# Eight experts in order of their load: three of them in 64-slot turns with the high and low parts in one stationary tile

## The chip, the cores and the metric

The kernel runs on one core of a Trainium2 chip. The metric is the device time of one execution in microseconds (us); lower is better. The median of three runs of the kernel before is 2497.24 us (2496.4 to 2498.56).

## The reference, cut to what matters

The model is two blocks of layers over 256 tokens of width 1024. The change lies in the mixture of experts of the first block:

```python
def moe_swiglu(xn, w_router, w_gate, w_up, w_down):     # N_EXPERTS 8, TOP_K 2, D_FF_EXPERT 3584
    logits = (xn @ w_router).astype(jnp.float32)
    top_v, top_i = lax.top_k(logits, TOP_K)
    top_w = jax.nn.softmax(top_v, axis=-1)
    gates = jnp.sum(jax.nn.one_hot(top_i, N_EXPERTS) * top_w[..., None], axis=-2)
    y = jnp.zeros_like(xn)
    for e in range(N_EXPERTS):
        y = y + gates[..., e:e + 1] * swiglu(xn, w_gate[e], w_up[e], w_down[e])
    return y
```

Each token goes to two of eight experts, so 512 places are filled, 64 for an expert on average. Counted with the reference's own inputs, experts 0 to 7 get 62, 71, 60, 74, 68, 59, 54 and 64 tokens.

## The kernel before, in words

All products are made of float32r matmuls on TensorE (PE). A number is split into a high part (rounded to float32r) and a low part (what is left), and a product takes three matmuls: high x high, high x low and low x high (`mm3`, lines 320 to 324). Weights come from HBM in chunks of 1 MB (`Stream`, lines 219 to 290). One chunk is 128 partitions x 2048 columns, and is split as two *parts* of 1024 columns: ScalarE (ACT) copies a part into `whi` (line 272), then VectorE (DVE) subtracts that copy from the raw weights and writes `wlo` (line 273). There are five pairs of `whi` and `wlo`, so a part can be converted only when PE is done with the part five before it. The raw chunks of the experts have 4 + 3 + 4 = 11 buffers. SyncE (SP) issues all these loads on one queue, in order of use, each when a buffer is free.

The router (line 816) gives each token a slot in each of its two experts; `weigh` makes the gates and the largest load, which is read into registers. `gather` (line 886) multiplies the tokens with one-hot tiles, for two experts at a time: 32 matmuls of 256 columns, after which `xgh` and `xgl` hold the transposed rows of up to 128 slots of either expert.

`experts` (line 913) takes the experts 0 to 7 one after the other, each over 128 slots. An expert has 14 *steps* j of 256 hidden columns. A step has two chunks of up and gate weights (four parts), whose 24 matmuls of 512 moving columns go into a bank `mm`; the slots' rows are the stationary operand, the weights move. Then ACT takes the silu of one half (line 941), DVE multiplies it by the other (line 942), PE transposes the result (line 946, two matmuls), and ACT and DVE split it into `hh` and `hl`. The down projection of the step before (one chunk, two parts, 12 matmuls into `acc`) follows in the program. At the end of an expert `acc` is split into `yh` and `yl` and put back to the tokens by eight matmuls (line 962) and four additions on DVE (line 964). In the last expert the parts are converted in halves of 512 columns (line 268).

A scheduler at build time sets the order of each engine's instructions, across the program's own order. On the chip each engine keeps to that order: an instruction that waits holds up all that stand behind it on its engine. If any load is over 128, a second pass over all eight experts takes the slots from 129 on (line 986); it does not run with these loads.

Of the kernel before, what the change touches and what calls it, by code (L numbers as in the profile page):

```python
# [11 lines left out]
F32 = mybir.dt.float32  # L12
# [10 lines left out]
NB = T // P  # L23
# [153 lines left out]
# ---------------------------------------------------------------- constants of the shapes  # L177

def constants():
# [12 lines left out]
    c["before"] = np.stack([np.triu(np.ones((P, P)), 1), np.ones((P, P))], axis=1)  # L192
    c["iota"] = np.broadcast_to(np.arange(1, P + 1)[None, :], (P, P))
    a = np.arange(P)
# [22 lines left out]
# ---------------------------------------------------------------- the program  # L217

class Stream:
    """Weights in the order of use: loaded ahead, then split into two float32r parts."""  # L220

    def __init__(self, prog, plans, raw_bufs, hl_bufs, raw_pool, hl_pool):
        self.nc = prog.nc
        self.items, self.parts, self.first = [], [], []
        for ap, plan in plans:
            offs, _ = offsets(plan)
            for c, o in zip(plan, offs):
                self.first.append(len(self.parts))
                step = max(c.kt // 2, 1)
                self.parts += [(len(self.items), k, step) for k in range(0, c.kt, step)]  # L230
                self.items.append((ap, c, o))
        self.first.append(len(self.parts))
# [6 lines left out]
    def widen(self, pool, bufs, until):  # L239
        """More room for raw chunks up to the one of the key `until`."""  # L240
# [5 lines left out]
    def fill(self, most=None):  # L246
        while self.n_raw < min(len(self.items), most or len(self.items)):
# [6 lines left out]
            step = f if self.n_raw else f // 2  # L254
            for c0 in range(0, f, step):
                self.nc.sync.dma_start(t[:, c0:c0 + step], bass.AP(tensor=ap.tensor, offset=ap.offset + o + c0, ap=[[f, P], [1, step]]))
# [24 lines left out]
    def get(self, *keys):  # L281
        """The rows of the next chunks, 128 at a time: a list of hi, lo [128, n]."""
# [10 lines left out]
class Program:  # L293
    RAW, HL = 4, 5

    def __init__(self, tc, io, stop=None, dump=None):
# [3 lines left out]
        self.turns = {}  # L300

    # -- small helpers

    def pool(self, name, bufs=1, **kw):
        """A tile pool whose tiles wait only for the earlier users of their own bytes."""
# [3 lines left out]
    def banks(self, **uses):  # L309
        """Which of the eight banks of PSUM each use takes in turn."""  # L310
# [24 lines left out]
    def inv_rms(self, ss, n, scale):  # L335
        """(ss * scale + eps) ** -0.5 on [128, n] sums of squares."""
# [7 lines left out]
    def row_rms(self, h, b, r):  # L344
        """r[:, b] = 1 / rms of the rows of block b of h."""
# [9 lines left out]
    def transposed(self, dst, src, b, kt):  # L355
        """dst hi/lo [128, kt, 256][:, :, block b] from src [128, kt * 128]."""
# [12 lines left out]
    def turned_h(self, gain, out, by_half=False):  # L369
        """h times the gain, transposed and split."""  # L370
# [7 lines left out]
    def normed_T(self, gain, by_half=False, pool=None):  # L378
        """h times the gain, transposed and split, and the rows' 1 / rms, which the products take after."""
# [7 lines left out]
    def row_of(self, pool, r):  # L387
        """r [128, 2] of the tokens as a row on every partition, [128, 256]."""
# [7 lines left out]
    def lin_tok(self, xT, keys, n, use):  # L396
        """x @ W for one column range: use(b, psum[:, :n])."""
# [7 lines left out]
    def lin_feat(self, xT, key):  # L405
        """(x @ W).T for 256 columns: psum [128, 2, 256]."""
# [26 lines left out]
    def down(self, acc, hT, keys, first, last, scale=None, store=False):  # L433
        """acc[b][n] += hT.T @ W for chunks of rows; hT(k) gives hi, lo [128, 256]."""
# [15 lines left out]
    def residual(self, b, n, ps, scale):  # L450
        """h += ps, or ps times a number for each token."""
# [6 lines left out]
    def at(self, name):  # L458
        """True where a debugging run ends."""
# [5 lines left out]
    # -- the whole  # L465

    def run(self):
        nc, io = self.nc, self.io
        with ExitStack() as st, ExitStack() as self.later, \
# [7 lines left out]
            self.w = Stream(self, [(io["w1"], plan_first()), (io["we"], sum((plan_expert(e) for e in range(NE)), [])),  # L477
# [5 lines left out]
            nc.vector.memset(self.mhalf, -0.5)  # L483
# [1006 lines left out]
```

## Time and profile before

| | us |
|---|---|
| median of 3 runs | 2497.24 |
| fastest, slowest run | 2496.4, 2498.56 |
| span of the profiled execution | 2493.5 |
| PE busy | 2462.6 (99%) |
| PE weight loads busy | 2066.8 (83%) |
| DVE busy | 1893.2 (76%) |
| ACT busy | 1560.4 (63%) |
| DMA, share of 16 engines (largest queue) | 64.2% |

The profile has no other time of that execution than its span; the span is 3.7 us under the median of the runs. The busy shares are means over stages with different limits: the experts, from about 575 to 1582 us, are the longest stage, and the one in which DMA and DVE are busiest. A busy PE is one with a matmul in flight; how fast it goes is read from the distance between the starts of matmuls.

### The profile page before, as it was taken

To read this page: it belongs to the slowest core of one execution; us is meant where nothing else is said; L and a number is where in the kernel's file an instruction comes from. 1 tells how busy PE (TensorE), PEld (TensorE's weight loads), DVE (VectorE), ACT (ScalarE), POOL (GpSimd) and SP (SyncE) were. 2 spreads that over 40 slices of the span, in tenths; PEclk is the share of its full clock that TensorE was granted. 3 is DMA by queue.
4 is the path that set the end of the run, shared out by engine and by line. 5 is a ranking of instruction groups with operands and counts; after the bars stand their busy time and mean duration, and the time that the engine had idled before them with its cause. 6 is when DMAs were issued, how large, how long until landed. Compare 5 with 4: busy or idle time off the path is not lost. (4 is left out here: it accounts for less than half of the span.)

```text
span 2493.5 us, 35325 instructions
## 1 busy us (share of the span) xinstructions
PE 2462.6 (99%) x13280; PEld 2066.8 (83%) x13280; DVE 1893.2 (76%) x2926; ACT 1560.4 (63%) x2560; POOL 63.6 (3%) x105
## 2 busy tenths in 40 slices
PE   8999999999999999999999999899999999999999
PEld 6978998888878888878887877698779989877998
DVE  5656557659999988898888898878676567867655
ACT  6446556657877777777777777645745554564544
POOL 0000000000000000000000000100000000100000
PEclk9999999999999999999999999999999999999999
DMA  7445555557999898989898988534255554424553
GB/s 280 165 167 206 186 186 186 197 232 297 367 347 363 327 364 341 359 336 367 341 365 336 363 344 338 146 126 175 102 176 204 186 171 133 176 105 172 194 187 108
DMA packets 88244, 605.75 MB, mean 243 GB/s; under 512 B 10336, under 2 KB 12000, under 8 KB 17152
## 3 DMA queue, kind: packets, MB, share of 16 engines
q1 hardware_dynamic: 85648, 593.96, 64.2%
q0 software_dynamic: 2416, 9.44, 1.7%
q8 instruction: 107, 1.75, 0.3%
q14 instruction: 73, 0.60, 0.1%
HBM read 602.31 MB, written 1.05 MB: 242 GB/s over the span
## 5 line engine op out<-in xcount | busy, mean ns | idle before, releaser
L273 DVE TENSOR_TENSOR wlo<-wraw,whi 128x512 fp32r<-128x512 f32 (+1 forms) x1656 | 1382.9, 875 | 383.6 <-ACT whi L272 365.5
L272 ACT ACTIVATE whi<-wraw 128x512 fp32r<-128x512 f32 (+1 forms) x1656 | 1205.3, 776 | 471.0 <-PE mm L323 211.3
L322 PE MATMUL mm<-xth,whi 128*128 128x256 f32 x1296 | 366.2, 283 | 0.0
L324 PE MATMUL mm<-xth,wlo 128*128 128x256 f32 x1296 | 364.9, 282 | 0.9 <-DVE wlo L273 0.9
L323 PE MATMUL mm<-xtl,whi 128*128 128x256 f32 x1296 | 365.8, 282 | 0.0
L323 PE MATMUL mm<-wlo,xgh 128*128 128x512 f32 x896 | 356.9, 398 | 2.8 <-DVE wlo L273 1.8
L322 PE MATMUL mm<-whi,xgh 128*128 128x512 f32 x896 | 355.1, 397 | 0.0
L324 PE MATMUL mm<-whi,xgl 128*128 128x512 f32 x896 | 354.3, 395 | 0.0
L324 PE MATMUL acc<-whi,hl 128*128 128x512 f32 x792 | 316.7, 401 | 0.3 <-DVE hl L328 0.3
L323 PE MATMUL acc<-wlo,hh 128*128 128x512 f32 x792 | 314.8, 398 | 0.0
L322 PE MATMUL acc<-whi,hh 128*128 128x512 f32 x792 | 297.0, 397 | 0.5 <-ACT hh L327 0.5
L323 PEld LDWEIGHTS mm<-xtl,whi 128*128 128x128 f32 x1296 | 244.3, 189 | 4.2 <-issue 2.5
L322 PEld LDWEIGHTS mm<-xth,whi 128*128 128x128 f32 x1296 | 244.4, 189 | 2.9 <-issue 1.1
L324 PEld LDWEIGHTS mm<-xth,wlo 128*128 128x128 f32 x1296 | 244.5, 189 | 1.8 <-DVE wlo L273 1.1
L323 PE MATMUL mm<-wlo,xth 128*128 128x512 f32 (+2 forms) x592 | 232.9, 394 | 0.8 <-DVE wlo L273 0.8
L322 PE MATMUL mm<-whi,xth 128*128 128x512 f32 (+2 forms) x592 | 232.7, 393 | 0.3 <-ACT xth L327 0.2
L324 PE MATMUL mm<-whi,xtl 128*128 128x512 f32 (+2 forms) x592 | 229.8, 389 | 0.4 <-DVE xtl L328 0.4
L323 PEld LDWEIGHTS mm<-wlo,xgh 128*128 128x128 f32 x896 | 168.4, 188 | 48.4 <-DVE wlo L273 9.5
L322 PEld LDWEIGHTS mm<-whi,xgh 128*128 128x128 f32 x896 | 168.3, 188 | 39.6
L324 PEld LDWEIGHTS mm<-whi,xgl 128*128 128x128 f32 x896 | 168.4, 188 | 38.5
L322 PEld LDWEIGHTS acc<-whi,hh 128*128 128x128 f32 x792 | 148.8, 188 | 34.7 <-ACT hh L327 1.8
L324 PEld LDWEIGHTS acc<-whi,hl 128*128 128x128 f32 x792 | 148.7, 188 | 33.9 <-DVE hl L328 1.9
(375 smaller groups left out, 2602.1 us busy)
## 6 DMA issues: line engine op xcount, KB each, us to landing
wraw<-in_we_dram SPq DMA_DIRECT2D x336, 1024.0 KB, 5.5
wraw<-in_w_dram SPq DMA_DIRECT2D x218, 1024.0 KB, 4.8
wraw<-in_w_dram SPq DMA_DIRECT2D x4, 912.0 KB, 5.0
wraw<-in_w_dram SPq DMA_DIRECT2D x6, 512.0 KB, 3.7
bias<-in_rel_rows_dram POOLq DMA_DIRECT2D x4, 768.0 KB, 4.6
gain<-in_norm_ffn_dram POOLq DMA_DIRECT2D x2, 512.0 KB, 5.9
gn<-in_ret_gn_dram SPq DMA_DIRECT2D x4, 256.0 KB, 3.5
gain<-in_norm_ple_dram POOLq DMA_DIRECT2D x2, 512.0 KB, 6.0
```

The costliest lines, as they stand in the source:

```text
L272: self.nc.scalar.activation(h, src, AF.Copy)
L273: self.nc.vector.tensor_tensor(l, src, h.bitcast(F32), op=ALU.subtract)
L322: mm(out, l[0], r[0], start=start, stop=False)
L323: mm(out, l[0], r[1], start=False, stop=False)
L324: mm(out, l[1], r[0], start=False, stop=stop)
```

## The change: what it does

The experts are taken in *turns*. Turn 0 is always expert 0, and its weights are loaded as before. The other seven are ranked on the chip by their load; turns 2, 3, 5 and 6 take the four largest in falling order, turns 1, 4 and 7 the three smallest. Which expert a turn takes is read from SBUF into seven registers of SP, and each of the 294 loads of turns 1 to 7 has its address from such a register. Slots and gates are reordered by turn.

Turns 0, 2, 3, 5 and 6 are computed as before, over 128 slots (wide). Turns 1, 4 and 7 have room for 64 slots (narrow): the stationary tile holds the high parts of 64 slots in its first 64 columns and the low parts in the others, and a product is two matmuls (tile x `whi`, tile x `wlo`), so a step has 16 + 8 matmuls instead of 24 + 12. Rows 0 to 63 and 64 to 127 of the result must then be added. For `mm`, ACT copies the whole bank to SBUF (`cp`), and four float32 matmuls of 64 columns with `fold` (two identities on top of each other) add the two halves and transpose at once; silu, product and split then work on 128 x 128. For `acc` the one-hot tile has both halves, so putting the tokens back adds them. `gather` takes the turns in groups (0), (1, 2), (3, 4), (5, 6), (7). The second pass would run if a load were over its room (128 or 64).

```diff
+WIDE = (True, False, True, True, False, True, True, False)
+GROUPS = ((0,), (1, 2), (3, 4), (5, 6), (7,))
...
 # Stream.fill
-                self.nc.sync.dma_start(t[:, c0:c0 + step], bass.AP(tensor=ap.tensor, offset=ap.offset + o + c0, ap=[[f, P], [1, step]]))
+            if c.key[0] in ("eu", "ed"):
+                e = self.expert[c.key[1]] if c.key[1] else 0
+                src = ap[e:e + 1] if isinstance(e, int) else ap[bass.ds(e, 1)]
+                self.nc.sync.dma_start(t[:, :f], src[:, o:o + P * f].rearrange("o (p f) -> (o p) f", p=P))
...
 # router, weigh
+            nc.vector.tensor_copy(loads, total)
+            nc.vector.scalar_tensor_tensor(key, loads, float(NE), self.turn[:, 2], op0=ALU.mult, op1=ALU.subtract)
+            nc.vector.memset(key[:, 0:1], 1e6)
+            nc.vector.tensor_tensor(perm, pairs(key, 0), pairs(key, 1), op=ALU.is_gt)
+            nc.vector.tensor_reduce(rank, perm, axis=AX.X, op=ALU.add)
+            nc.vector.tensor_tensor(perm, pairs(rank, 0), pairs(self.turn[:, 0], 1), op=ALU.is_equal)
+            for i, t in enumerate((self.turn[:, 2], loads)):
+                nc.vector.tensor_tensor(part[:, 0], perm, pairs(t, 0), op=ALU.mult)
+                nc.vector.tensor_reduce(picked[:, i], part[:, 0], axis=AX.X, op=ALU.add)
+            nc.vector.tensor_copy(which, picked[:, 0])
+            for i in range(1, NE):
+                self.expert[i] = nc.values_load(which[0:1, i:i + 1], (mybir.EngineType.SP,), min_val=0, max_val=NE - 1)
...
+            def by_turn(i, t):
+                nc.vector.tensor_tensor(part, t[:, :, None, :].to_broadcast([P, NB, NE, NE]),
+                                        perm[:, None].to_broadcast([P, NB, NE, NE]), op=ALU.mult)
+                nc.vector.tensor_reduce(in_turn[:, i], part, axis=AX.X, op=ALU.add)
...
 # gather, of a group with a narrow turn (its last)
+            nc.scalar.activation(flat(xg[0][:, ks])[:, :, :cut], flat(ps)[:, :, :cut], AF.Copy)
+            if nw:
+                nc.vector.tensor_tensor(xg[1][:, ks, 0], ps[:, :, 0], xg[0][:, ks, 0].bitcast(F32), op=ALU.subtract)
+            nc.vector.tensor_tensor(xg[0][:, ks, nw, 64:], ps[:, :, nw, 64:], xg[0][:, ks, nw, :64].bitcast(F32), op=ALU.subtract)
...
 # experts
+            def product(out, x, wk, start, stop):
+                if wide[e]:
+                    self.mm3(out, x, wk, start, stop)
+                else:
+                    nc.tensor.matmul(out, x[0], wk[0], start=start, stop=False)
+                    nc.tensor.matmul(out, x[0], wk[1], start=False, stop=stop)
...
+                else:
+                    hT[j] = (hh,)
+                    cp = self.work.tile([P, 512], F32, name="cp", tag="xs", bufs=3)
+                    nc.scalar.activation(cp, ps, AF.Copy)
+                    tp = self.bank("tp")[:, :256].rearrange("p (c s) -> p c s", s=64)
+                    for c in range(4):
+                        nc.tensor.matmul(tp[:, c], cp[:, c * P:(c + 1) * P], self.fold, start=True, stop=True)
+                    sg = self.work.tile([P, 2, 64], F32, name="sgn", tag="xs", bufs=3)
+                    nc.scalar.activation(sg, tp[:, :2], AF.Silu)
+                    nc.vector.tensor_tensor(sg, sg, tp[:, 2:], op=ALU.mult)
+                    self.split_psum(hh[:, :, :64], hh[:, :, 64:], sg)
```

On ACT, one step of an expert in the middle of the stage reads so before (`sg` is the silu, `hh` the split of the step's result):

```order
L272 ACTIVATE whi<-wraw 128x1024 x4
L941 ACTIVATE sg<-mm 128x256
L272 ACTIVATE whi<-wraw 128x1024 x2
L327 ACTIVATE hh<-tp 128x256
L272 ACTIVATE whi<-wraw 128x1024 x3
```

and so in turn 4 of the change (`cp` is the copy of the bank, `sgn` the silu):

```order
L288 ACTIVATE whi<-wraw 128x1024 x5
L1025 ACTIVATE cp<-mm 128x512
L1030 ACTIVATE sgn<-tp 128x128
L288 ACTIVATE whi<-wraw 128x1024
L344 ACTIVATE hh<-sgn 128x2x64
```

The silu now stands right behind the copy, with PE's four `fold` matmuls between the two, and no conversion of weights between them. Counted through the stream, `cp` stands here behind the second part after the last of its own step, and so do the last five steps of turn 1; in the first seven steps of turn 1 it stands behind the fifth, with a conversion before the silu. In turn 7 it stands behind the second, again with a conversion before the silu.

On PE, around the transposes of a step before (`tp<-ident,sg`):

```order
L322 MATMUL acc<-whi,hh 128x512 x2
L323 MATMUL acc<-wlo,hh 128x512
L946 MATMUL tp<-ident,sg 128x128 x2
L324 MATMUL acc<-whi,hl 128x512
L323 MATMUL acc<-wlo,hh 128x512
```

and around the `fold` matmuls of turn 4 of the change:

```order
L994 MATMUL mm<-wlo,xgh 128x512
L993 MATMUL acc<-whi,hh 128x512 x2
L994 MATMUL acc<-wlo,hh 128x512
L1028 MATMUL tp<-fold,cp 128x64 x4
L994 MATMUL acc<-wlo,hh 128x512
```

Between the last matmul into `mm` and the fold stand three matmuls of the next part; the transposes before stood behind some nine.

On SP, at the start of the stage, before (`wraw` is a raw chunk, from `we`, the experts' weights; `load` is the largest load):

```order
L256 DMA wraw<-in_we_dram 128x2048 x10
L1029 DMA lb_in<-in_lb_t_dram 128x8
L256 DMA wraw<-in_we_dram 128x2048
L983 TENSOR_LOAD load
L983 ISA x2
L256 DMA wraw<-in_we_dram 128x2048 x324
```

and in the change, where the row pair of `which` stands seven times:

```order
L267 DMA wraw<-in_we_dram 128x2048 x10
L1115 DMA lb_in<-in_lb_t_dram 128x8
L267 DMA wraw<-in_we_dram 128x2048 x2
L873 TENSOR_LOAD which
L873 ISA x2
L1068 TENSOR_LOAD load
L1068 ISA x2
L267 DMA wraw<-in_we_dram 128x2048 x29
L267 ISA
```

Seven register loads are new, one chunk later than the one that was there, and from turn 1 on a register instruction stands ahead of every load.

## Rows read from the trace of the kernel before

**Rows 1.** Busy time by stretch, about one expert each: engines, clock, DMA share, GB/s.
```profile
575.00:700.00 125.00, 125.00 (x563) 100.69 (x562) 114.47 (x125) 100.43 (x120) 0.00 (x0) 1.00 0.92 349
951.00:1077.00 126.00, 126.00 (x573) 101.85 (x572) 112.07 (x122) 93.13 (x119) 0.00 (x0) 1.00 0.91 344
1455.00:1580.00 125.00, 122.66 (x526) 94.38 (x524) 113.39 (x198) 95.63 (x192) 0.00 (x0) 1.00 0.73 286
```

**Rows 2.** Line 964, the additions that end each expert: first and last start.
```profile
L964 DVE SCALAR_TENSOR_TENSOR h<-ps,gates,h x32: 740/744/751, 699.4 to 1582.3; 128x512 f32<-128x512 f32 x32
```

**Rows 3.** DVE timeline in the first expert's end: start, us, instructions.
```profile
702.46 1.40 DVE L964 SCALAR_TENSOR_TENSOR h<-ps,gates,h 128x512 f32<-128x512 f32 x2
703.78 3.49 DVE L273 TENSOR_TENSOR wlo<-wraw,whi 128x1024 fp32r<-128x1024 f32 x3
```

**Rows 4.** PE timeline, matmuls of one expert in order of start.
```profile
640.31 0.39 PE L324 MATMUL mm<-whi,xgl 128*128 128x512 f32 x1
640.54 0.40 PE L322 MATMUL acc<-whi,hh 128*128 128x512 f32 x1
640.78 0.39 PE L323 MATMUL acc<-wlo,hh 128*128 128x512 f32 x1
```

**Rows 5.** ACT timeline of one step of the same expert.
```profile
640.74 0.39 ACT L941 ACTIVATE sg<-mm 128x256 f32<-128x256 f32 x1 [0.33 <-PE mm L324]
641.02 2.18 ACT L272 ACTIVATE whi<-wraw 128x1024 fp32r<-128x1024 f32 x2
...
649.36 0.39 ACT L941 ACTIVATE sg<-mm 128x256 f32<-128x256 f32 x1 [0.34 <-PE mm L324]
```

**Rows 6.** Groups of instructions by line and form, 600 to 1500 us: busy us, mean ns.
```profile
L273 DVE TENSOR_TENSOR wlo<-wraw,whi 128x1024 fp32r<-128x1024 f32 x570 | 671.0, 1220 | 51.9 <-ACT whi L272 46.3 <-DMA wraw<-in_we_dram 1.6
L272 ACT ACTIVATE whi<-wraw 128x1024 fp32r<-128x1024 f32 x569 | 574.7, 1054 | 43.3 <-PE mm L324 32.1 <-PE acc L324 6.4 <-DMA wraw<-in_we_dram 1.0
L942 DVE TENSOR_TENSOR sg<-sg,mm 128x256 f32<-128x256 f32 x100 | 41.8, 418 | 30.0 <-ACT sg L941 30.0
L941 ACT ACTIVATE sg<-mm 128x256 f32<-128x256 f32 x101 | 38.9, 385 | 143.8 <-PE mm L324 143.7
L900 PE MATMUL ps<-oh,xth 128*128 128x256 f32 x48 | 9.9, 282 | 0.0
L328 DVE TENSOR_TENSOR yl<-acc,yh 128x512 fp32r<-128x512 f32 x14 | 9.6, 685 | 0.4 <-ACT yh L327 0.4
L327 ACT ACTIVATE yh<-acc 128x512 fp32r<-128x512 f32 x14 | 8.1, 596 | 5.8 <-PE acc L324 5.8
```

**Rows 7.** DVE and ACT timelines in the last expert.
```profile
1485.55 6.11 DVE L273 TENSOR_TENSOR wlo<-wraw,whi 128x512 fp32r<-128x512 f32 x10
...
1484.89 5.31 ACT L272 ACTIVATE whi<-wraw 128x512 fp32r<-128x512 f32 x10
```

**Rows 8.** PE timeline of the second block: eight float32 matmuls of 64 columns.
```profile
1656.80 1.00 PE L1377 MATMUL sb<-q,k 128*128 128x64 f32 x8
```

**Rows 9.** The smallest instructions of ACT and DVE near 573 us.
```profile
572.67 0.19 ACT L838 ACTIVATE w<-w 128x2 f32<-128x2 f32 x1
...
572.27 0.17 DVE L882 SCALAR_TENSOR_TENSOR slot<-ps,u 128x16 f32<-128x16 f32 x1 [1.08 <-PE ps L880]
573.38 0.15 DVE L835 CAST load<-most 128x1 int32<-128x1 f32 x1
573.45 0.16 DVE L840 RECIPROCAL w<-w 128x2 f32<-128x2 f32 x1
```

**Rows 10.** SP timeline: loads issued around the register load.
```profile
575.23 0.33 SPq L256 DMA_DIRECT2D wraw<-in_we_dram  x1
...
584.16 0.33 SPq L256 DMA_DIRECT2D wraw<-in_we_dram  x1
```

**Rows 11.** What SP's queue waited for, 600 to 1500 us: total us, times, longest.
```profile
SPq L256 <- DVE wlo L273: 494.7, 205, 6.6
SPq L256 <- DVE hl L328: 245.6, 71, 4.3
SPq L256 <- DVE sg L942: 69.6, 25, 4.0
```

**Rows 12.** Busy time in two stretches with the DMA engines full.
```profile
836.00:856.00 20.00, 20.00 (x89) 16.10 (x88) 19.39 (x21) 15.96 (x20) 0.00 (x0) 1.00 1.00 394
1100.00:1120.00 20.00, 20.00 (x90) 16.17 (x89) 17.50 (x21) 14.29 (x18) 0.00 (x0) 1.00 1.00 354
```

More of the change, by code (lines that the diff above doesn't have):

```diff
@@ L191, in constants @@
     c["decay"] = dec
-    c["before"] = np.stack([np.triu(np.ones((P, P)), 1), np.ones((P, P))], axis=1)
+    c["before"] = np.triu(np.ones((P, P)), 1)
     c["iota"] = np.broadcast_to(np.arange(1, P + 1)[None, :], (P, P))
+    wide = [i for i in range(NE) if WIDE[i]]
+    turn = wide + [i for i in range(NE) if not WIDE[i]]
+    rank = [turn.index(i) for i in range(NE)]
+    room = [P if w else P // 2 for w in WIDE]
+    c["turns"] = np.broadcast_to(np.array([rank, room, range(NE)], np.float64)[None], (P, 3, NE))
     a = np.arange(P)
@@ L830, in weigh @@
             for b in range(NB):
-                nc.tensor.matmul(total, before[:, 1, :], sel[:, b, :], start=b == 0, stop=b == 1)
+                nc.tensor.matmul(total, self.one.to_broadcast([P, P]), sel[:, b, :], start=b == 0, stop=b == 1)
+            loads = pool.tile([P, NE], F32, name="loads")
+            nc.vector.tensor_copy(loads, total)
+            key = pool.tile([P, NE], F32, name="key")
+            nc.vector.scalar_tensor_tensor(key, loads, float(NE), self.turn[:, 2], op0=ALU.mult, op1=ALU.subtract)
@@ L846, in weigh @@
             nc.vector.tensor_tensor(gates, gates, sel, op=ALU.add)
-            return gates, load
+            return by_turn(1, gates), slots, load
         def parts(b):
@@ L910, in gather, with experts @@
+        ohT = pool.tile([P, n, T], F32R, name="ohT", bufs=2)
         nc.scalar.activation(ohT, tp, AF.Copy)
-        return xg, ohT
-    def experts(self, px, pool, gates, slot, w, first):
+        return {i: ([x[:, :, a] for x in (xg if wide[i] else xg[:1])], ohT[:, a]) for a, i in enumerate(turns)}
+    def experts(self, px, pool, gates, slot, w, first, wide):
         nc = self.nc
-        pair = {0: first}
+        have = dict(first)
         nj = FFE // 256
+        groups = {g[0]: g for g in GROUPS[1:]}
@@ L948, in experts @@
                 if 0 < j < nj - 1:
                     down(j - 1)
-            if ei and e2 + 1 < NE // 2:
-                pair[e2 + 1] = self.gather(px, pool, slot, e2 + 1)
+            if e + 1 in groups:
+                have.update(self.gather(px, pool, slot, groups[e + 1], wide))
             down(nj - 2, nj - 1)
@@ L980, in moe_layer @@
                     quarter(1, 1)
-                gates, load = weigh()
+                gates, slot, load = weigh()
                 self.lb = self.lower_bounds(pool)
-                most = nc.values_load(load[0:1, 0:1], min_val=0, max_val=T)
-                self.experts(px, pool, gates, slot, self.w, first)
+                most = nc.values_load(load[0:1, 0:1], min_val=0, max_val=P + T)
+                self.experts(px, pool, gates, slot, self.w, first, WIDE)
         self.wide.close()
@@ L988, in moe_layer @@
                     self.pool("hl2", 4) as hl, self.banks(acc="67", mm="45", tp="01", ps="23"):
-                again = Stream(self, [(io["we"], sum((plan_expert(e) for e in range(NE)), []))], 2, 4, raw, hl)
-                nc.vector.tensor_scalar(slot, slot, float(P), None, op0=ALU.subtract)
-                self.experts(pool, pool, gates, slot, again, self.gather(pool, pool, slot, 0))
+                again = Stream(self, [(io["we"], plan_expert(i)) for i in range(NE)], 2, 4, raw, hl)
+                nc.vector.tensor_tensor(slot, slot, self.turn[:, None, 1].to_broadcast([P, NB, NE]), op=ALU.subtract)
+                wide = (True,) * NE
+                self.experts(pool, pool, gates, slot, again, self.gather(pool, pool, slot, GROUPS[0], wide), wide)
         self.routed.close()
@@ L1466, in device_inputs @@
     arrays["w1"] = packed(plan_first(), inputs)
-    arrays["we"] = packed(sum((plan_expert(e) for e in range(NE)), []), inputs)
+    arrays["we"] = packed(sum((plan_expert(e) for e in range(NE)), []), inputs).reshape(NE, -1)
     arrays["w2"] = packed(plan_second(), inputs)
```

108 lines of the change are left out of this document (68 added, 40 removed).

## Prediction, made before the changed kernel was run

> **What bounds the kernel now.** I read the busy time by stretch first. In an expert's 125 us PE is busy all the time, DVE 112 to 114 us of it, ACT 93 to 100, and the DMA engines 0.91 to 0.92 of it [rows 1]: PE is the limit, but DVE is within 11% and the loads within 9%. The length of an expert comes from line 964, its closing additions: the first expert's last pair starts at 702.46 [rows 3], so its last one at 703.1, and the eighth expert's last at 1582.3 [rows 2]; (1582.3 - 703.1) / 7 = 125.6 us. The timelines give the beat: matmuls of 512 columns start 0.233 us apart [rows 4], 36 of them make 8.4 us, and the step from one silu to the next is 649.36 - 640.74 = 8.62 us [rows 5]. The groups say who waits: ACT stands 143.7 us in 101 silus until PE ends `mm`, about 1.4 us each [rows 6], so it is PE that sets the beat. SP's queue waits for a free buffer for 494.7 + 245.6 + 69.6 = 810 of 900 us [rows 11]: the eleven buffers are full.
>
> **What a narrow turn takes away.** On PE 168 of 504 matmuls go, 168 x 0.233 = 39 us, and 28 transposes. The four folds of a step are float32 matmuls of 64 columns, of which eight take 1.00 us when they follow each other [rows 8]: spacing 0.104, four in 0.58 us with the drain, 8 us in a turn. So PE needs 24 x 0.233 + 0.42 = 6.0 us for a step instead of 8.62. What it needs no longer decides; the weights still have to be converted, all of them, and the conversions do not shrink with the slots.
>
> *DVE in a narrow step.* Three `wlo` in a row take 3.49 us [rows 3], 1.14 each, so six take 6.8. The product and the split shrink from 128x256 (0.42 us [rows 6]) to 128x128, which no row shows: between 0.17 (16 columns [rows 9]) and 0.42; I take 0.27 at its full length and 0.22 queued, nearer the smaller since half the columns go. Sum 7.2 us. *ACT in a narrow step:* two `whi` take 2.18 us [rows 5], the mean is 574.7 / 569 = 1.01, six take 6.1; the copy `cp` is 128x512 out of PSUM like `yh`, 0.60 [rows 6]; silu and `hh` lie between 0.19 [rows 9] and 0.385 [rows 6], 0.28 each. Sum 7.2. Two engines at 7.2 that hand work to each other, and to PE, will not both run without a gap, so I follow one step round the ring.
>
> *The ring in turn 4.* Time 0 is the end of the `wlo` of the last part that `mm` needs. PE has three matmuls left, 3 x 0.233 and 0.17 of drain: 0.9. `cp` to 1.5. The folds stand behind three matmuls of the next part, whose `wlo` ends at 1.14, so they wait for `cp`, not for these: 2.1. Silu to 2.4. Behind it on ACT stands the next `whi`: 3.4. In these 3.4 us DVE had two `wlo` to do (to 2.3) and the product (from 2.4 to 2.7), and then it waits for that `whi`. `wlo` to 4.6, the split to 4.8, three more `wlo` to 8.25. Eight handovers at 0.04 (PE's `mm` ends at 640.70, the silu starts at 640.74 [rows 4, 5]) add 0.3: 8.5 us, against 8.62 of a wide step. DVE's 7.2 is stretched by 1.3, because ACT stands still between copy and silu while the folds run and has only conversions behind it.
>
> *Turn 1.* In its first nine steps `cp` stands three to five parts behind, mostly five, with a conversion ahead of the silu. The fifth `whi` needs the pair that PE frees at 0.9: it ends at 1.9, `cp` at 2.5, folds at 3.1, the conversion between at 3.55, silu at 3.85; DVE has three `wlo` to do (3.4) and waits only 0.45; product, three `wlo` and split bring it to 7.75. The last five steps are like turn 4. *Turn 7.* Conversions go in halves: ten on DVE take 6.11 us, ten on ACT 5.31 [rows 7], so a step has 12 x 0.61 + 0.45 = 7.75 on DVE and 12 x 0.53 + 1.1 = 7.5 on ACT. The silu has a conversion before it and DVE three parts, so the folds' time is covered: 7.75.
>
> *The ends of a turn* cost DVE four additions at 0.70 [rows 3] and two `yl` queued at 0.6 (0.685 alone [rows 6]): 4.0 us, in all three. Turn 4 also has a gather behind it, 8 small splits and 4 one-hots on DVE, about 2 us.
>
> | turn | steps | ends | us | saved of 125.6 |
> |---|---|---|---|---|
> | 1 | 9 x 7.75 + 5 x 8.5 = 112.3 | 4.0 | 116.3 | 9.3 |
> | 4 | 14 x 8.5 = 119.0 | 6.0 | 125.0 | 0.6 |
> | 7 | 14 x 7.75 = 108.5 | 4.0 | 112.5 | 13.1 |
>
> Together 23.0 us.
>
> **What it adds.** *Ranking:* some 22 small instructions more on DVE between the slots and the first product. Independent ones follow each other at 0.07 (573.38 to 573.45), dependent ones take their full 0.16 [rows 9]: 1.5 to 3.7 us; the first gather's tiles are half as wide and give back about 1. I take 2 us, all exposed, since PE's first products wait for DVE there; bounds 0 and 4. *Gathers:* one more, but that of turn 4 lies where PE has room, so four stand on PE's path as before, two of them with 128 instead of 256 columns. A pair of 256-column ones costs 32 x 0.12 = 3.8 us (spacing half the 0.233 of 512 columns; 0.282 alone [rows 6]). No row has 128 columns of float32r: half or double, so -4 to +4; I take 0. *Register loads on SP:* eight instead of one. The one before was ready to read at 573.5 (`load`, [rows 9]) and the next chunk was issued at 575.23 [rows 10]: at most 1.7 us each, 13 for eight, at least 0. The chunk that they now delay was issued at 584.16 [rows 10], and `which` is written near 579, so the delay is 0 to 8 us, up to three chunks of a lead of eleven, in a wide turn that PE bounds: nothing, as long as the lead holds. The Trainium skill, "DMA: Bandwidth & Descriptors", section "Latency and other measured facts", gives a floor of about 0.6 us for such a load; by that it would be an estimated 5 us of SP and the same sum; no row here isolates one.
>
> Sum: 23.0 - 2 = 21 us. The span becomes 2493.5 - 21 = 2472.5, and with the 3.7 us by which the runs' median lies above the span, **2476 us**. Its own range, from folds that take 0.3 more or less a step and the bounds above: 2464 to 2488.
>
> **Rivals.**
> *The converters run without gaps.* For it: DVE was busy 19.39 of 20 us in one stretch [rows 12], so it can. Then turns take 14 x 7.2 + 4 = 104.8, 106.8 and 112.5, saving 20.8 + 18.8 + 13.1 = 52.7, less 2: 2446. Against it: the order on ACT, where nothing can pass the silu. Chance 0.16.
> *The loads become the bound.* A chunk is 1.049 MB and an expert 42 of them, 44.04 MB. With the engines full the trace has 394 GB/s in one stretch and 354 in another [rows 12]: 111.8 or 124.4 us an expert. At their mean, 118.1, a narrow turn of the forecast is at most 5.6 us ahead of its loads, two chunks of the lead, which wide turns refill. If 354 is what lasts and the lead is lost at the start, each narrow turn takes 124.4, saves 1.2, and the sum is 3.6 - 2: 2496. Chance 0.11. The Trainium skill, "DMA: Bandwidth & Descriptors", Specifications, has a limit of about 358 GB/s per core on the HBM side: by it an expert's weights take an estimated 123 us and the time would be some 2491. The stretch with 394 GB/s disagrees with it as a ceiling for this core.
> *The ring is longer than a wide step: slower.* One place, ACT between `cp` and silu in turns 1, 4 and 7. With folds that do not overlap (4 x 0.27 = 1.1, from the 0.27 that is left of 1.00 after seven spacings), a silu of 0.385 and a `whi` of 1.09 a step is 8.5 + 0.5 + 0.1 + 0.1 = 9.2. From 8.85 on in all three turns the kernel is slower than before ((125.6 + 2.3 - 4.0) / 14); at 9.2 in all a turn takes 132.8 and the time is 2497 + 21.6 + 2 = 2521. For it: no row has this ring. Against it: rows 8 show the folds' kind overlapped. Chance 0.09.
> *Not what it says.* Addresses from registers could be slow to issue; a chunk must come every 125.6 / 42 = 2.99 us, and an issue takes 0.33 [rows 10]; at 3.3 the 294 loads would cost 91 us. Or the second pass runs, over 900 us more; with the reference's counts the three smallest of experts 1 to 7 are 60, 59 and 54, under 64, and the largest 74. Chance 0.04 for both.
>
> **How the numbers follow.** Forecast 0.60, converters 0.16, loads 0.11, ring 0.09, the last 0.04. The range 2445 to 2497 holds the forecast, nearly all of the first and the second rival, and leaves out the rest, 0.2. About 0.2%, 5 us, is what a measurement of this kernel can tell. Faster by more: nearly all of 0.60, 0.16 and a little of the loads, 0.78. Within: the loads and the edge of the forecast, 0.11. Slower: 0.11.
>
> **What would show it.** Right: `wlo` x6 per narrow step in distances of 7.7 to 8.5 us, ACT idle before `sgn` behind PE's fold by 0.5 us or more in each step of turn 4, turn 4 the longest narrow turn and turn 7 the shortest; PE idle before `mm` behind `wlo`, DMA at 350 to 390 GB/s. Wrong: narrow turns all alike near 105 us (no ring), or near 124 with SP waiting for nothing and `whi` waiting for DMA (loads), or a gap of PE after 580 us behind SP's register loads.

## The result, and the profile after

| | before | after |
|---|---|---|
| median of 4 runs, us | 2496.82 (2496.1 to 2498.56) | 2464.86 (2464.25 to 2466.75) |
| ratio | | 0.9874, 95% interval 0.986 to 0.9888 |
| span of the profiled execution | 2493.5 | 2462.5 |

32.0 us less, where the prediction had 21. The range of 2445 to 2497 holds it; of the likeliest case's own range, 2464 to 2488, it is the lower end. The sign came out, and the number is half as large again. That it lies so near is luck: the narrow turns gave less than forecast, the additions cost more, and 20 us came from something that the forecast does not contain, as the following shows.

The closing additions (line 1049 now) cut the span as they did before [rows 2]. First and last start in the kernel after:

```profile
L1049 DVE SCALAR_TENSOR_TENSOR h<-ps,in_turn,h x32: 739/743/752, 699.5 to 1561.9; 128x512 f32<-128x512 f32 x32
```

| | before | after | difference |
|---|---|---|---|
| up to turn 0's last addition | 703.1 | 703.2 | 0 |
| turn 1 | 127.2 | 118.3 | -8.9 |
| turns 2, 3 | 124.3, 126.1 | 124.9, 124.3 | -1.2 |
| turn 4 | 125.2 | 127.0 | +1.8 |
| turns 5, 6 | 126.0, 123.9 | 124.1, 124.1 | -1.7 |
| turn 7 | 126.4 | 116.0 | -10.4 |
| behind the experts | 911.2 | 900.7 | -10.5 |

Turn 4 is the longest narrow turn and turn 7 the shortest, as forecast, but all three are longer than forecast (116.3, 125.0, 112.5), and turn 4 is longer than a wide turn. The busy times of turns 1, 2, 4 and 7, which answer to [rows 1]; the columns are the same:

```profile
703.00:821.00 118.00, 107.23 (x464) 74.17 (x463) 106.17 (x119) 96.88 (x128) 0.00 (x0) 1.00 0.98 373
821.00:946.00 125.00, 124.98 (x573) 101.61 (x572) 111.99 (x126) 93.36 (x119) 0.00 (x0) 1.00 0.92 350
1070.00:1197.00 127.00, 114.81 (x492) 76.56 (x492) 108.55 (x123) 99.10 (x134) 0.00 (x0) 1.00 0.90 344
1445.00:1561.00 116.00, 109.44 (x450) 68.91 (x449) 111.34 (x200) 100.52 (x209) 0.00 (x0) 0.99 0.80 309
```

In turn 4 no engine is full (PE 114.8, DVE 108.6, ACT 99.1 of 127 us) and the DMA engines are at 0.90: a ring of waits, not an engine. One step of it on ACT (start, us, line, instruction, and in brackets the idle time before and what ended it), the answer to [rows 5]:

```profile
1112.31 0.60 ACT L1025 ACTIVATE cp<-mm 128x512 f32<-128x512 f32 x1 [0.99 <-PE mm L994]
1114.10 0.28 ACT L1030 ACTIVATE sgn<-tp 128x128 f32<-128x128 f32 x1 [1.20 <-PE tp L1028]
1114.27 1.05 ACT L288 ACTIVATE whi<-wraw 128x1024 fp32r<-128x1024 f32 x1
1115.22 0.30 ACT L344 ACTIVATE hh<-sgn 128x128 fp32r<-128x128 f32 x1
1115.42 4.84 ACT L288 ACTIVATE whi<-wraw 128x1024 fp32r<-128x1024 f32 x5
1121.24 0.60 ACT L1025 ACTIVATE cp<-mm 128x512 f32<-128x512 f32 x1 [0.98 <-PE mm L994]
1123.04 0.28 ACT L1030 ACTIVATE sgn<-tp 128x128 f32<-128x128 f32 x1 [1.20 <-PE tp L1028]
```

The silus are 1123.04 - 1114.10 = 8.94 us apart, the forecast had 8.5. On PE and DVE in the same step:

```profile
1112.96 1.10 PE L1028 MATMUL tp<-fold,cp 128*128 128x64 f32 x8
...
1116.64 0.51 PE L994 MATMUL mm<-wlo,xgh 128*128 128x512 f32 x1 [0.77 <-DVE wlo L289]
```

```profile
1114.41 0.29 DVE L1031 TENSOR_TENSOR sgn<-sgn,tp 128x128 f32<-128x128 f32 x1 [0.89 <-ACT sgn L1030]
1115.36 1.23 DVE L289 TENSOR_TENSOR wlo<-wraw,whi 128x1024 fp32r<-128x1024 f32 x1 [0.66 <-ACT whi L288]
```

The ring is the one of the prediction, station by station: PE's folds, ACT's silu behind them, DVE behind the silu and then behind the next `whi`, PE behind `wlo`. Its longer station is the folds: the program has four of them, the trace shows eight records in 1.10 us. The waits of turns 1 to 7 (total us, times, longest) say the same:

```profile
PEld mm L994 <- DVE wlo L289: 74.6, 153, 1.1
DVE wlo L289 <- ACT whi L288: 41.4, 76, 1.7
ACT sgn L1030 <- PE tp L1028: 35.4, 41, 1.3
```

The surprise lies where nothing was changed. Wide steps are 8.54 us long, not 8.62 [rows 5], and of the 31 us in the two spans 10.5 come behind the experts. In the second block, PE's products of 512 columns with the same tiles, two starts of a run without a gap, first of the kernel before and then of the one after:

```profile
1904.68 0.39 PE L322 MATMUL acc<-whi,hh 128*128 128x512 f32 x1
...
1907.48 0.40 PE L322 MATMUL acc<-whi,hh 128*128 128x512 f32 x1
```

```profile
1881.44 0.39 PE L339 MATMUL acc<-whi,hh 128*128 128x512 f32 x1
...
1884.16 0.39 PE L339 MATMUL acc<-whi,hh 128*128 128x512 f32 x1
```

From the first start to the last are twelve distances: 2.80 / 12 = 0.233 us before, 2.72 / 12 = 0.227 after, at a granted clock of 1.00 (2.4 GHz) in both stretches. What differs is where the tiles lie. `one`, 32 bytes of each partition with its padding, stands ahead of the tiles of the dense layers and of the second block; the experts' own tiles (`xgh`, `xgl`, `hh`, `hl`) lie behind the router's tables, of which `turns` and `fold` are new and one is smaller.

### The profile page after: what moved, and what is told of

It reads as the page before. It is cut to its first block, busy times and chain, and to the rows that moved or that the text cites. A ratio compares the mean times of both kernels' runs of the same rounds, so it can differ in the third digit from the quotient of the medians.

```text
span 2462.5 us, 35589 instructions
## 1 busy us (share of the span) xinstructions
PE 2402.0 (98%) x13060; PEld 1987.3 (81%) x13060; DVE 1880.3 (76%) x2964; ACT 1564.7 (64%) x2607; POOL 61.3 (2%) x105
## 5 line engine op out<-in xcount | busy, mean ns | idle before, releaser
L341 PE MATMUL acc<-whi,hl 128*128 128x512 f32 x624 | 247.1, 397 | 0.4 <-DVE hl L345 0.4
L340 PE MATMUL acc<-wlo,hh 128*128 128x512 f32 x624 | 245.0, 393 | 0.0
L339 PE MATMUL acc<-whi,hh 128*128 128x512 f32 x624 | 231.7, 391 | 0.0
L340 PE MATMUL mm<-wlo,xgh 128*128 128x512 f32 x560 | 222.8, 398 | 1.6 <-DVE wlo L289 1.6
L341 PE MATMUL mm<-whi,xgl 128*128 128x512 f32 x560 | 221.4, 395 | 0.0
L994 PE MATMUL mm<-wlo,xgh 128*128 128x512 f32 x336 | 148.3, 441 | 20.2 <-DVE wlo L289 17.5
L341 PEld LDWEIGHTS acc<-whi,hl 128*128 128x128 f32 x624 | 117.2, 188 | 24.0 <-DVE hl L345 1.7
L339 PEld LDWEIGHTS acc<-whi,hh 128*128 128x128 f32 x624 | 117.3, 188 | 23.5 <-ACT hh L344 0.8
L340 PEld LDWEIGHTS acc<-wlo,hh 128*128 128x128 f32 x624 | 117.4, 188 | 21.2 <-DVE wlo L289 0.3
```

Source lines behind the costliest of these rows:

```text
L339: mm(out, l[0], r[0], start=start, stop=False)
L340: mm(out, l[0], r[1], start=False, stop=False)
L341: mm(out, l[1], r[0], start=False, stop=stop)
L994: nc.tensor.matmul(out, x[0], wk[1], start=False, stop=stop)
```

## Experiments on the addresses

Each ratio below is to the kernel before, run beside it; its medians lie between 2495.19 and 2496.82 us, so differences of 1 to 2 us between kernels of different sessions say little.

**The kernel before, tiles moved by 32 bytes.**

```diff
+            self.pad = self.keep.tile([P, 8], F32, name="pad")
...
+            pad2 = self.plep.tile([P, 8], F32, name="pad2")
```

> The kernel before, with one unused tile of 32 bytes per partition behind `mhalf` and one in the pool of the router's tables: nothing else, and the same order on every engine. All tiles behind them (xth, xtl, hh, hl, xgh, xgl, whole pools) then start on a multiple of 64 bytes, as in the changed kernel; in the kernel before they start 32 bytes past one. Theory A (the 1% in stages the change does not touch comes from these addresses): matmuls of 512 columns in the second block start 0.227 to 0.230 us apart and not 0.233, the step of a wide expert is 8.54 and not 8.62 us, and the kernel takes 2496.8 - 7 (ahead of the experts) - 8 x 1.1 (experts) - 10.6 (behind them) = about 2470 us. Theory B (another order of instructions, another code layout, or removed work does it): 2497, spacing 0.233.

2476.3 us against 2495.88 of before: 0.992 (0.9907 to 0.9934). 900.9 us behind the experts, not 911.2, and the products of above:

```profile
1881.97 0.39 PE L322 MATMUL acc<-whi,hh 128*128 128x512 f32 x1
1882.20 0.39 PE L323 MATMUL acc<-wlo,hh 128*128 128x512 f32 x1
1882.43 0.39 PE L324 MATMUL acc<-whi,hl 128*128 128x512 f32 x1
1882.65 0.39 PE L322 MATMUL acc<-whi,hh 128*128 128x512 f32 x1
```

1882.65 - 1881.97 = 0.68 for three, 0.227. Theory A: 19.6 us for two unused tiles. It is 6 less than worked out, since the wide step came to 8.59 and not to 8.54: the experts' tiles start on multiples of 64 here too, but not at the same places as in the changed kernel. The chains below tell why that counts.

**The changed kernel, tiles moved back.**

```diff
-            self.one = self.keep.tile([P, 1], F32, name="one")
+            self.one = self.keep.tile([P, 16], F32, name="one")[:, :1]
...
-            self.fold = self.plep.tile([P, 64], F32, name="fold")
+            self.fold = self.plep.tile([P, 72], F32, name="fold")[:, :64]
```

> The changed kernel with `one` given 64 bytes per partition and not 32, and `fold` 32 bytes more, so that all tiles behind them start 32 bytes past a multiple of 64 again, as in the kernel before; the same order on every engine. Theory A (addresses): +7 ahead of the experts, +10.6 behind them, +1.1 in each of five wide turns, about 0 in the narrow ones, where PE is not the limit: 2465 + 23 = about 2488 us. Theory B: 2465.

2485.2 us: 0.9955 (0.9942 to 0.9969). The wide step is 8.61 to 8.63 again, and 913.9 us pass behind the experts. So the four kernels make a square:

| us | tiles as before | tiles moved by 32 bytes |
|---|---|---|
| experts as before | 2495.9 | 2476.3 |
| experts as changed | 2485.2 | 2464.9 |

Moving the tiles is worth 20 us in either kernel, and the written change 10.7 us at the old addresses. The 11.4 us of the right column are not at equal addresses: the experts' tiles of the kernel before still lie worse there (wide step 8.59 for 8.54), 14 x 8 x 0.05 = 5.6 us. An estimate for the kernel before with its tiles where the changed kernel has them is 2476.3 - 5.6 = 2470.7, and then the written change is worth some 6 us there. (In the left column the changed kernel's tiles are not at the very places of before within 256 bytes either, but the products start as far apart: in the second block the means are 118.8 and 118.7 ns for 256 columns with `xth`, 234.2 and 233.7 for 512 with `hh`.)

**The spacing by itself.** Chains of products with no other engine at work; the loop, for 512 columns (a first pass over the same places, not shown, takes all stationary operands from one tile):

```python
for mo in MOVE:                # 0, 32, 64, 128 bytes
    for so in STAT:            # 0, 32, ... 480 bytes
        for i in range(12):
            nc.tensor.matmul(ps, s[so][:, i % 4 * P:(i % 4 + 1) * P], m[mo][:, i % 2 * 512:(i % 2 + 1) * 512],
                             start=i == 0, stop=i == 11)
```

> The disputed cost by itself: nothing of the reference, only chains of float32r matmuls with no other engine at work. 12 of 512 columns for each of 16 start addresses of the stationary tile (0, 32, ... 480 bytes past a multiple of 512: sA, sB, ... sP) and four of the moving tile (0, 32, 64, 128 past one: mA, mB, mC, mE); then 16 of 256 columns with the two roles exchanged. Theory alignment (each tile's own distance to a multiple of 64 or 128 decides): with mA the chains of sA, sE, sI, sM are the fastest and all others alike; the same four whatever the moving tile. Theory difference (the two addresses against each other decide, as the four kernels together suggest: hh at the same phase of 512 as whi 0.227 us, 32 bytes before it 0.233, 128 behind it 0.232; xth 256 behind 0.227, 192 behind 0.229 to 0.232): with mB the fastest is sB and sJ, with mC sC and sK. Theory neither (contention with the other engines' accesses makes the difference): all 64 chains alike at 0.227 or below.

The chains of 512 columns with the stationary tiles sG to sJ (192, 224, 256, 288 bytes) against mA (0), and then of 256 columns with sG to sI as the moving one:

```profile
219.81 2.92 PE L62 MATMUL acc<-mA,sG 128*128 128x512 f32 x12
222.57 2.96 PE L62 MATMUL acc<-mA,sH 128*128 128x512 f32 x12
225.36 2.89 PE L62 MATMUL acc<-mA,sI 128*128 128x512 f32 x12
228.09 2.95 PE L62 MATMUL acc<-mA,sJ 128*128 128x512 f32 x12
230.88 2.96 PE L62 MATMUL acc<-mA,sK 128*128 128x512 f32 x12
...
392.61 1.99 PE L71 MATMUL mm<-sG,mA 128*128 128x256 f32 x16
394.44 2.05 PE L71 MATMUL mm<-sH,mA 128*128 128x256 f32 x16
396.32 2.08 PE L71 MATMUL mm<-sI,mA 128*128 128x256 f32 x16
398.24 2.05 PE L71 MATMUL mm<-sJ,mA 128*128 128x256 f32 x16
```

From one chain's start to the next, sI takes 2.73 us and sJ 2.79; sG takes 1.83 and sI 1.92. Within the chains (first start to last), with one address taken from the other modulo 256 bytes:

| difference, bytes | 0 | 32 | 64 | 96 | 128 | 160 | 192 | 224 |
|---|---|---|---|---|---|---|---|---|
| 512 columns, stationary - moving: ns | 227 | 233 | 234 | 233 | 232 | 234 | 230 | 233 |
| 256 columns, moving - stationary: ns | 120 | 118 | 118 | 119 | 119 | 117 | 115 | 118 |

The row is the same for all four moving tiles, so it is the difference that counts, with a period of 256 bytes. The exceptions: of the 16 chains of 512 columns at a difference of 0 (both passes) three have 230, and of the 8 of 256 columns at 192 one has 118. Multiples of 64 or 128 as such mean nothing. `whi` and `wlo` lie 128 past a multiple of 256 in all these kernels, so each operand's place in the table can be worked out from the program's addresses: `hh` of the second block went from 224 to 0 (233 to 227), `xth` from 160 to 192 (as stationary tile 234 to 230, as moving one 117 to 115), the experts' `hh` from 160 to 0 (234 to 227), their `xgh` from 32 to 128 (233 to 232). All four moved to a better place, by chance. The kernel before with moved tiles has `xth` and the second block's `hh` at the places of the changed kernel, but the experts' `hh` at 192 (230) and their `xgh` at 64 (234): hence its 8.59.

## Experiments on the narrow turns

**All turns wide.**

```diff
-WIDE = (True, False, True, True, False, True, True, False)
+WIDE = (True,) * 8
```

> The changed kernel with all eight turns wide: ranking, register loads, addresses and the groups of gathers stay, the narrow path goes. If the narrow turns give only what lies between them and an aligned wide turn of 124.4 us: turns 1, 4 and 7 change from 118.3, 127.0 and 116.0 to 124.4, 124.4 and 125.5, +13: about 2478 us. If the narrow turns are the whole gain: 2497. The difference between this kernel and the one before with aligned tiles is then the price of ranking and gathers, forecast at 2 us; from the trace I expect 5 to 8.

2477.32 us: 0.9925 (0.9912 to 0.9939). So the narrow turns give 2477.3 - 2464.9 = 12.4 us at these addresses, where a wide turn is shorter than the 125.6 us of the forecast; the forecast had 23. Turn by turn wide and narrow: 121.8 and 118.3, 125.0 and 127.0, 125.3 and 116.0. Turn 4 loses 2 by being narrow. (Turn 2 was 127.0 here and 124.9 in the changed kernel, which makes up most of the rest.) Against the kernel before with moved tiles it is 1.0 us slower, not 5 to 8; but its experts' tiles lie better (wide step 8.54 for 8.59), and those 5.6 us hide the price: ranking and gathers cost 1.0 + 5.6 = 6.6 us by this estimate, as expected from the trace.

**Half the folds.**

```diff
-                    for c in range(4):
+                    for c in range(2):
...
-                    nc.vector.tensor_tensor(sg, sg, tp[:, 2:], op=ALU.mult)
+                    nc.vector.tensor_tensor(sg, sg, tp[:, :2], op=ALU.mult)
```

> The changed kernel with two of the four fold matmuls in each narrow step: it leaves out the folds of the up half (the product takes the gate half twice). The trace shows the four folds as eight matmuls in 1.00 to 1.10 us, where the prediction took 0.58. Theory ring with folds of 1.1: the steps of turn 4 go from 8.94 to about 8.4 and the turn from 127.0 to 119.5; turns 1 and 7 gain less, some 3 each: about 2452. Rival, the converters or the loads set the step: 2465, steps of turn 4 at 8.9.

2461.07 us: 0.9864 (0.9849 to 0.9879). Turn 4, whose order stayed, is what was asked:

```profile
1115.28 0.28 ACT L1030 ACTIVATE sgn<-tp 128x128 f32<-128x128 f32 x1 [0.75 <-PE tp L1028]
...
1123.77 0.28 ACT L1030 ACTIVATE sgn<-tp 128x128 f32<-128x128 f32 x1 [0.75 <-PE tp L1028]
```

8.49 us a step with two folds (four records in 0.66 us), and the turn 121.4: the ring of the prediction, with the folds' time that the prediction gave to four. Turn 1 fell to 113.4. Turn 7 did not follow, 121.2 us instead of 116.0: with the cheaper folds the scheduler put no conversion between its copies and silus, ACT stands 1.53 us there, and the step went from 8.09 to 8.72. That is a second view of the same ring; my total of 2452 missed it.

**The ring opened.**

```diff
-                    nc.scalar.activation(cp, ps, AF.Copy)
+                    nc.scalar.activation(cp, ps, AF.Copy); w._split()
...
-                    nc.scalar.activation(sg, tp[:, :2], AF.Silu)
+                    with self.tc.issue_after(w.conv.ins): nc.scalar.activation(sg, tp[:, :2], AF.Silu)
```

(`w.conv` is the last `whi`.)

> The changed kernel with the ring opened: in a narrow step a conversion of the next part is recorded behind the copy `cp`, and the silu is issued behind it, so ACT converts (two parts in turn 4) while PE folds. Theory ring (ACT standing 1.2 us behind the folds in each step sets 8.94 us): the steps of turn 4 fall to about 7.6, turn 4 to about 112, the last four steps of turn 1 by 1.3 each: about 2465 - 15 - 5 = 2445. Theory loads (turn 1 already has the DMA engines 0.98 busy at 373 GB/s, so 118 us an expert is the floor): turn 4 falls to 118 to 119 and turn 1 stays: about 2456. If ACT's idle time is not what sets the step: 2465.

2442.58 us: 0.9788 (0.9775 to 0.9801), 22.3 us less than the change. Turns 1, 4 and 7 take 113.5, 116.1 and 113.7 us, their steps mostly 7.4 to 7.8. (Turn 4 had been put at 112; its steps are 7.74 and not 7.6, and turn 5 fell from 124.1 to 121.7 besides.) ACT in turn 4, and the busy times of turn 1:

```profile
1110.71 0.60 ACT L1025 ACTIVATE cp<-mm 128x512 f32<-128x512 f32 x1 [0.41 <-PE mm L994]
1111.20 2.00 ACT L288 ACTIVATE whi<-wraw 128x1024 fp32r<-128x1024 f32 x2
1113.10 0.27 ACT L1030 ACTIVATE sgn<-tp 128x128 f32<-128x128 f32 x1
```

```profile
703.00:816.00 113.00, 106.83 (x464) 75.46 (x463) 107.22 (x120) 96.22 (x129) 0.00 (x0) 0.98 0.98 398
```

The silu waits for nothing any more: ring shown. The loads were not the floor either: 398 GB/s over a whole turn. The limit of about 358 GB/s in the Trainium skill ("DMA: Bandwidth & Descriptors", Specifications), which the prediction weighed, is there half of what two cores share. For one core at work alone, as here, the 398 GB/s show that it is no ceiling.

**All operands on multiples of 128 bytes.** On the opened kernel:

```diff
-            self.one = self.keep.tile([P, 1], F32, name="one")
+            self.one = self.keep.tile([P, 24], F32, name="one")[:, :1]
...
+            self.pad = pool("pad", 1).tile([P, 16], F32, name="pad")
```

> The changed kernel with the ring opened, and two unused tiles more so that nearly every tile that PE reads as a float32r operand starts on a multiple of 128 bytes; so far xth and xtl, the operands of all dense layers, started 64 bytes past one. Nothing else, the same order. Theory 64 (a multiple of 64 bytes is all that counts): 2442.6, unchanged. Theory 128 (the wide step was 8.54 us with the experts' tiles on multiples of 128, 8.59 where they lay 64 bytes past one, 8.62 at 32 bytes): the matmuls with xth and xtl go from 0.230 to 0.227 us for 512 columns and from 0.1175 to 0.114 for 256; some 1,300 and 3,600 of them make 4 and 12 us: 2427 to 2432.

2452.11 us, 0.9829 (0.9815 to 0.9842): 9.5 slower, my theory of alignment was wrong. This run came ahead of the chains, and gave the clue to them: in the medians ahead of the experts, 512 columns with `xth` went from 0.230 to 0.227, but 256 columns from 0.117 to 0.120 and the products with `hh` from 0.227 to 0.232. With the table: `xth` came to a difference of 0, the best for one use and the worst for the other, and `hh` to 128.

**The addresses chosen by the table.** On the opened kernel, 128 bytes ahead of `xgl` and `xgh` and 128 more ahead of `hh`:

```diff
+                pads = [q.tile([P, 32], F32, name="pad") for q in (px, pool)]
```

> The changed kernel with the ring opened, and two unused tiles of 128 bytes: one ahead of xgl and xgh, one ahead of hh and hl. The experts' xgh and xgl then lie at the same place within 256 bytes as whi and wlo (before: 128 away), and hh and hl stay where they are within 256; all else stays. Theory difference (the chains measured by themselves: 0.227 us at a difference of 0 within 256 bytes, 0.232 at 128): 24 of the 36 products of a wide step start 0.005 us closer, the step goes from 8.54 to about 8.42 us, five wide turns of 14 steps give 8.4 us, the narrow turns nothing (the conversions set them): 2442.6 - 8 = about 2434 us. Theory 128 (multiples of 128 bytes are all alike): 2442.6.

2433.97 us: 0.9753 (0.974 to 0.9766), the fastest, 30.9 under the change and 8.6 under the opened kernel. The wide step:

```profile
862.30 0.39 ACT L1015 ACTIVATE sg<-mm 128x256 f32<-128x256 f32 x1 [1.97 <-PE mm L341]
...
870.72 0.39 ACT L1015 ACTIVATE sg<-mm 128x256 f32<-128x256 f32 x1 [1.97 <-PE mm L341]
```

8.42 us, as worked out; the narrow steps stayed at 7.4 to 7.8.

## Experiments on the ranking and the gathers

**The order written into the program.**

```diff
+            ORDER = (0, 2, 1, 3, 5, 4, 7, 6)
+            self.expert.update(enumerate(ORDER))
...
-            return by_turn(1, gates), slots, load
+            return gates, slot, load
```

> The changed kernel with the order of the experts written into the program (0, 2, 1, 3, 5, 4, 7, 6) and not found on the chip: no ranking on DVE, no seven register loads on SP, constant addresses; narrow turns, gathers and tile addresses stay. It leaves out the check that the small loads fit in 64 slots. Theory of the prediction (the ranking costs 2 us, register loads nothing): 2463. Theory from the traces (PE stands 0.9 us and runs small matmuls only, and its granted clock then is 0.5 for 6.8 us, which costs about 3 more): 2459 to 2460, and no stretch at half clock near 570 us. If address registers slow the loads: below 2455.

2466.97 us: 0.9887 (0.9872 to 0.9902), not faster than the change. (The written order has experts 1 and 3 the other way round than the ranking puts them; both turns are wide.) Turn 0 ends at 702.57, 0.6 us sooner, and all later turns are equal to the changed kernel's within 0.1 us. But the lead is there before the ranking: the slots, which both kernels make alike, are written at

```profile
564.91 0.17 DVE L933 SCALAR_TENSOR_TENSOR slot<-ps,u 128x16 f32<-128x16 f32 x1 [1.06 <-PE ps L931]
```

```profile
564.17 0.17 DVE L933 SCALAR_TENSOR_TENSOR slot<-ps,u 128x16 f32<-128x16 f32 x1 [1.07 <-PE ps L931]
```

in the changed kernel and with the written order. From there to the end of turn 0 it is 138.3 and 138.4 us. So the ranking and the seven register loads cost nothing that these traces show. The 2.9 us more lie behind the experts, with one more stretch of 3.4 us at half the clock there. The half clock near 570 us stayed, with PE standing 1.27 us ahead of it and not 0.88.

**The same with four pairs of gathers.**

```diff
-GROUPS = ((0,), (1, 2), (3, 4), (5, 6), (7,))
+GROUPS = ((0, 1), (2, 3), (4, 5), (6, 7))
```

> The kernel with the order of the experts written into the program, and the gathers in four pairs, (0, 1), (2, 3), (4, 5), (6, 7), as in the kernel before, and not in five groups with turn 0 alone; the narrow turns stay. It leaves out the check that the small loads fit in 64 slots. In the kernel with the written order the ranking turned out to cost 0.7 us, but the first expert ended 5.4 us later than with four pairs and aligned tiles, and PE's granted clock was 0.54 from 567 to 574 us, while it gathered turn 0 alone with matmuls of 128 columns. Theory gather (one gather more and the stretch at half clock that the small first one brings): no half clock near 570 us, and 4 to 6 us less than with the written order alone: 2461 to 2463. Theory move (the first expert's loss is only a gather that moved from turn 1 into turn 0): 2467, the half clock perhaps gone.

2465.12 us (2461.81 to 2466.99): 0.9876 (0.9859 to 0.9892). The granted clock at the start of the first products, of the changed kernel, of the written order and of four pairs (the column ahead of the DMA share):

```profile
568.00:575.00 7.00, 6.52 (x24) 5.85 (x25) 5.84 (x29) 1.17 (x4) 0.00 (x0) 0.51 0.40 150
```

```profile
567.00:574.00 7.00, 5.73 (x22) 5.24 (x22) 4.06 (x17) 1.31 (x4) 0.00 (x0) 0.54 0.39 151
```

```profile
567.00:574.00 7.00, 7.00 (x40) 6.04 (x39) 6.71 (x20) 4.79 (x7) 0.00 (x0) 1.00 0.50 163
```

With the first pair gathered at once PE stays busy and at 2.4 GHz, turn 0 ends at 694.08 instead of 702.57, and the experts as a whole 7.4 us sooner. From the slots to the end of turn 0 the difference is 8.2 us. Of these, 4.6 are there at the first product (3.1 us behind the slots, and 7.7 with turn 0 alone); the others fit the second gather, which falls into turn 0 with five groups and into turn 1 with four, and turn 1 takes 121.2 us here and not 118.3.

A gather of one turn is also hardly shorter than one of two. Its 32 matmuls have 128 columns instead of 256, but start about as far apart; first the changed kernel, then the kernel before, two matmuls to a row:

```profile
565.87 0.39 PE L958 MATMUL ps<-oh,xtl 128*128 128x128 f32 x2
566.09 0.39 PE L958 MATMUL ps<-oh,xth 128*128 128x128 f32 x2
```

```profile
573.76 0.40 PE L900 MATMUL ps<-oh,xth 128*128 128x256 f32 x2
574.00 0.40 PE L900 MATMUL ps<-oh,xtl 128*128 128x256 f32 x2
```

That is 0.11 us for 128 columns and 0.12 for 256.

The profiled execution is the fastest of the four, its span 4.8 us under that of the written order: 7.4 sooner in the experts, 2.6 more behind them. In the medians 1.9 us are left, within the spread of the runs. So the grouping costs 7.4 us at its place in the two traces, and in the total it is not shown. What passes behind the experts goes with the time at half clock there: 899.6 to 900.9 us in the five kernels with 6.8 us of it (the changed one, the one before with moved tiles, all wide, opened, and addresses chosen), 903.1 and 903.6 with 3.4 us more (half the folds, written order), 906.2 with two stretches of 6.8. Why these stretches differ from kernel to kernel was not tried.

## Why the prediction was right, and what in it was not

- **The bound.** Right: PE sets the wide step and not the narrow one, and no engine is full in a narrow one. The loads as the bound (2496) and converters without gaps (2446) are out: the opened kernel and ACT's 35 us before `sgn` show it.
- **The ring of turn 4.** Right in every station, wrong in one size. "Four in 0.58 us with the drain" came from the eight records of [rows 8], read as eight instructions. The trace shows two records for each such matmul, so four folds take 1.0 to 1.1, and 8.5 becomes 8.94. Two folds gave 8.49 and the opened ring 7.74.
- **The narrow turns' sum.** 23.0 forecast. At the old addresses, where the 125.6 us of before are the measure, turns 1 to 7 take 861.0 us against 879.2: 18.2. The rest is the folds' time, in turn 4, in turn 7 (8.09 for 7.75) and in turn 1 (7.9 for 7.75, and 8.94 for 8.5 in its last four steps). The rival with the longer ring was half true: turn 4 passed its threshold of 8.85 and lost 2 us; turns 1 and 7, which have a conversion between copy and silu in most steps or in all, did not. The threshold itself was added up wrongly: with 2 us of additions, three such turns cost time from (125.6 - 0.67 - 4.0) / 14 = 8.64 on, and turn 4 with its ends of 6.0 from 8.54 on.
- **What it adds.** Two us for the ranking were too many (nothing shows), the register loads at nothing were right. "Gathers: I take 0" failed: at the old addresses turn 0 ends 6.2 us later than before, and 7.6 later counted from the slots (138.4 us for 130.8). Narrower columns gave nothing back, and the forecast counted instructions and not that a gather of one turn alone leaves PE standing and at half clock, nor that the second gather falls into turn 0.
- **What was not in it.** The addresses: 20 us. "Addresses" appeared only as those of the loads. Nobody who counts instructions sees this term; the diff has it in its new tiles, `one` for the dense layers and the second block, `turns`, `fold` and a smaller table for the experts.

So the sum at the old addresses was -10.7 us and not -21. (The profiled spans have -9.3: -18.2, + 6.2, and 2.7 more behind the experts, where this kernel has 3.4 us more at half clock.) The 20 us of the addresses brought the total to 32, 11 past the forecast on the other side. The range would have held 2485 us too, but that the time lies only 11 us from the forecast comes of two errors of opposite sign, which is luck; the forecast's own sum was twice too large.

## What to carry to other kernels

When stages that a change does not touch change their time, compare the distance between starts of the same instructions first, and then the addresses: two unused tiles of 32 bytes tell within one run. Two kernels are at equal addresses only if each pair of operands has the same difference modulo 256; "moved by as much" is not enough. Count a row's records against the program's instructions before a price is taken from it. An engine that only hands a result on (a copy, then a function behind another engine's work) wants independent work recorded between the two, and that is worth trying before any smaller tile is.

## What the runs showed of the hardware

- Products of float32r start 0.227 to 0.234 us apart for 512 columns, 0.115 to 0.120 for 256, with the difference of the two operands' SBUF addresses modulo 256 bytes; 0 is the best for 512 columns and the worst for 256, 192 the best for 256 (the chains). What in the chip makes it was not tried.
- Matmuls of 128 columns in the gather start 0.11 us apart, those of 256 columns 0.12.
- A float32 matmul of 64 columns leaves two records (336 for the 168 folds of the changed kernel), and four of them take 1.10 us.
- One core, alone at work, drew 398 GB/s over 113 us.
- The granted clock fell to one half (1.2 GHz) for 6.8 us, from 568.1, while PE stood 0.88 us in the gather of one turn alone; with a pair gathered at once it stayed at 2.4 GHz. The standing alone does not make it: in the kernel before PE stood 1.13 us near 562, and the clock stayed at 2.4 GHz. What else it takes was not tried. The rows, of the changed kernel and of the kernel before:

```profile
568.48 0.69 PE L958 MATMUL ps<-oh,xth 128*128 128x128 f32 x2 [0.88 <-DVE xgl L345]
```

```profile
563.27 1.23 PE L863 MATMUL tp<-ident,xg 128*128 128x128 f32 x8 [1.13 <-DVE xg L859]
```
